# Two of four forgetting heads in query halves, and TensorE in the program's order from the merge on

## The chip, the core and the metric

One NeuronCore of a Trainium2 chip runs the whole program. It has a matrix engine (TensorE, PE in the profile), a vector engine (VectorE, DVE), an activation engine (ScalarE, ACT), GpSimd (POOL), and a queue engine that issues the transfers (SyncE, SP). Each engine works through its own list of instructions. The metric is device microseconds of one execution, the median of three runs.

## The reference, cut to what matters

```python
def token_mixer(h, w_in, b_forget, w_up_a, w_up_b, w_out):
    z = h @ w_in
    qa, ka, va, qb, kb, vb, fz, gza, gzb = jnp.split(z, SPLIT_POINTS, axis=-1)
    ya = dilated_mixture(qa, ka, va) @ w_up_a             # branch A: 12 heads, 3 groups of 4
    yb = forgetting_attention(qb, kb, vb, fz, b_forget) @ w_up_b   # branch B: 4 heads
    merged = jax.nn.sigmoid(gza) * ya + jax.nn.sigmoid(gzb) * yb
    return merged @ w_out

def one_block(args):                                      # of branch B: 128 queries of every head
    i, qi, Fi = args
    s = jnp.einsum('bqhd,bkhd->bhqk', qi, k).astype(jnp.float32) * scale
    s = s + (Fi[..., :, None] - F[..., None, :])
    qpos = i * BLOCK + jnp.arange(BLOCK)
    s = jnp.where(kpos[None, :] <= qpos[:, None], s, -jnp.inf)
    p = jax.nn.softmax(s, axis=-1)
    return jnp.einsum('bhqk,bkhd->bqhd', p.astype(v.dtype), v)
```

2048 tokens, 1024 channels, all in float32. Before `token_mixer` stands a normalisation, behind it a residual add, a gated feed-forward layer and a last normalisation.

## The kernel before

The program runs in stages: the input projection, the two attention branches with the merge, the output projection, and the feed-forward layer. The change lies in the second one.

**Branch A** (`branch_a`, `head_a`) handles one head after the other: scores, softmax without its division, sums. A head ends with its results in DRAM (`u_scr`, `den_scr`, `sta_scr`). **Branch B** (`branch_b`, `head_f`) handles a head in blocks of 128 queries. `half_tiles` loads the head's queries `qs`, keys in a high and a low part `kh` and `kl`, and values `vhl` (for keys 0 to 1023 packed into two tiles, `kk` and `qv`). `scores(cq, b)` handles one block of 128 queries, in segments of up to 512 keys: two matmuls into `psX` or `psZ`, one DVE instruction that adds the bias and takes the running maximum (the profile's L853, followed by a short read of the accumulator), then ACT's exponentials (L863). `sums(cq)` handles 256 queries. For every pair `kp` of key blocks it transposes four 128x128 pieces on PE into `psT` (L887), lets ACT copy them as the high part `ph` (L104) and DVE subtract to get the low part `pl` (L105), and then multiplies the values with both on PE into `psY` (L895), four matmuls in the order ph, pl, ph, pl. In this text four transposes, the copy, the subtraction and four matmuls are a block pair. A head's second half (queries 1024 to 2047) has 5, 6, 7 and 8 of them, so 26.

**Merge and first products.** When branch A is done, `merge_weights` turns its statistics into weights, through DRAM (`wrow`). `up(cp)` then handles a half of the 2048 tokens: it loads results of both branches and the weights into tiles `uw`, makes the operands `y` (split in high and low again), and multiplies them with `w_up_a` and `w_up_b` into `psZ` (L98 to L100: 12 matmuls a step), where DVE multiplies with the gates `gt` (L1017). `up(0)` needs every head's first half of queries, `up(1)` the second half.

**Order.** All of this is written as generators, and `together` draws steps from two of them in turn: each step yields a cost, a factor stretches it, and the generator with the lower clock goes next. Branch A against branch B goes with `PACE[0]`, and `up(0)` against what is left of B with `PACE[1]`. The framework's scheduler takes the instructions in that order as a priority and fixes each engine's own list when the program is built, by a model of its own; so an engine's list can differ from the order in which the code issues. Inside `tc.manual_schedule(engines={...})` the engine named there keeps the program's order.

Before, B runs all four heads over the first half of the queries and then all four over the second half. The merged stretch (up(0) with B) begins when the four first halves are done (`f_done` at 8), with the second halves to go, of which head 0's is nearly done and head 1's begun when branch A ends. Tiles are drawn from pools with a fixed number of slots: 11 of tag `big` (8 KiB a partition; q, k, v and y), 3 of `bigx` (`uw`), 2 buffers for each of `psX`, `psY`, `psZ`, `psT`.

## Time and profile before

| | us |
|---|---|
| median of three runs | 2924.74 (2924.5 to 2925.12) |
| the profiled execution, its own time | 2925.13 |
| its span, first to last instruction | 2923.4 |
| end of branch A (its last store is issued) | 1159.6 |
| end of branch B (its last product ends) | about 1375 |
| end of up(1) | about 1442 |

The time outside the span is 1.7 us. Times inside are counted from the span's start. The stage of the change is the stretch from 876 us, where the last products of the input projection give way to the two branches, to 1442 us. A profile's busy share of PE counts each matmul from its start to its modelled end, so two matmuls in flight overlap; the spacing of their starts tells what each costs.

### The profile page before, as it was taken

The numbers are of one execution on the slowest core, as the hardware profiler recorded it, in microseconds if no ns is written. First come the engines' busy times: TensorE is split into PE (matmuls) and PEld (weight loads), VectorE is DVE, ScalarE is ACT, GpSimd is POOL, SyncE is SP. The second block draws the span as 40 slices with busy tenths as digits, with TensorE's granted clock in tenths as the row PEclk, the third lists the DMA queues.
The fourth block names the chain that finished last, engine by engine and source line by source line (L and its number), as shares of the span: only waits on it lengthen the run. The fifth ranks groups of instructions, "written<-read, shape, count | busy, mean of one in ns | idle before, by whom it ended". The sixth has DMA issues, their size and how long they took to land.

```text
span 2923.4 us, 40639 instructions
## 1 busy us (share of the span) xinstructions
PE 2761.3 (94%) x13666; PEld 2286.0 (78%) x13666; DVE 2059.2 (70%) x4295; ACT 1378.0 (47%) x2722; POOL 184.3 (6%) x291
## 2 busy tenths in 40 slices
PE   5899999999999988787899999999999999989998
PEld 4689888978888877675677788888888888868876
DVE  7765578576547877886877866657755558786987
ACT  4654345344447767555255633334433335343543
POOL 0000000000002222342300000000000000000000
PEclk8999999999999999999899999999999999999999
DMA  7587476467858885965856654444522235685642
GB/s 252 155 218 226 130 214 197 152 173 203 247 182 288 271 207 165 277 214 179 287 174 206 211 169 134 136 159 126 173 80 83 80 114 180 211 259 170 219 152 98
DMA packets 527321, 538.89 MB, mean 184 GB/s; under 512 B 91876, under 2 KB 376956, under 8 KB 521212
## 3 DMA queue, kind: packets, MB, share of 16 engines
q1 hardware_dynamic: 527112, 536.30, 59.1%
q8 instruction: 107, 1.75, 0.3%
q14 instruction: 102, 0.84, 0.1%
HBM read 364.89 MB, written 171.29 MB: 183 GB/s over the span
## 4 chain that ended last, share of the span: by engine, by line
PE 48%; DMA 5%; DVE 4%; issue 1%; ACT 1%; SPq 0%; POOLq 0%; POOL 0%; DVEq 0%; ACTq 0%
PE psX L98 9%; PE psX L99 9%; PE psX L100 9%; PE psZ L98 5%; PE psZ L99 5%; PE psZ L100 5%; PE psY L99 2%; PE psY L98 2%; PE psY L100 2%; DMA uw<-wrow 1%; DMA wr<-in_w_up_b_dram 1%; PE psY L895 1%; DMA kl<-qk 0%; PE psX L851 0%; DMA h2sp<-pe 0%
## 5 line engine op out<-in xcount | busy, mean ns | idle before, releaser
L104 ACT ACTIVATE wh<-wt 128x512 fp32r<-128x512 f32 (+1 forms) x464 | 288.5, 623 | 630.8 <-PE psX L99 332.4
L105 DVE TENSOR_TENSOR wl<-wt,wh 128x512 fp32r<-128x512 f32 (+1 forms) x464 | 314.5, 681 | 258.4 <-ACT wh L104 240.4
L104 ACT ACTIVATE wh<-wr 128x512 fp32r<-128x512 f32 (+1 forms) x324 | 201.5, 623 | 454.1 <-PE psX L99 254.1
L105 DVE TENSOR_TENSOR wl<-wr,wh 128x512 fp32r<-128x512 f32 (+1 forms) x324 | 220.0, 680 | 193.1 <-ACT wh L104 172.2
L215 DVE TENSOR_TENSOR wt<-wr 128x512 f32<-128x512 f32 (+1 forms) x216 | 146.6, 679 | 11.9 <-DMA wr<-in_w_in_dram 5.6
L215 DVE TENSOR_TENSOR wt<-wr,wt 128x512 f32<-128x512 f32 (+1 forms) x216 | 147.1, 681 | 3.7
L242 ACT ACTIVATE u<-psX 128x512 f32<-128x512 f32 x216 | 125.6, 581 | 8.6 <-PE psX L100 7.6
L839 POOL TENSOR_SCALAR bi<-nf,F_col 128x512 f32<-128x512 f32 (+3 forms) x160 | 106.4, 667 | 260.3 <-DVE mx L853 210.5
L863 ACT ACTIVATE L<-L,nmf 128x512 f32<-128x512 f32 (+3 forms) x160 | 103.4, 648 | 27.1 <-DVE nmf L859 26.8
L104 ACT ACTIVATE ph<-psT 128x512 fp32r<-128x512 f32 (+1 forms) x126 | 71.3, 573 | 69.4 <-PE psT L887 67.4
L1123 DVE TENSOR_TENSOR ac<-psZ,u 128x512 f32<-128x512 f32 x88 | 60.5, 688 | 42.2 <-PE psZ L100 41.2
L105 DVE TENSOR_TENSOR pl<-psT,ph 128x512 fp32r<-128x512 f32 (+1 forms) x126 | 81.5, 653 | 9.8 <-ACT ph L104 9.4
L797 PE MATMUL psY<-pf,va 128*65 128x128 f32 (+1 forms) x408 | 78.9, 328 | 3.2 <-DVE nm L764 1.1
L769 ACT ACTIVATE L<-L,nm 128x128 f32<-128x128 f32 (+1 forms) x192 | 72.5, 450 | 18.9 <-DVE nm L764 17.6
L887 PE MATMUL psT<-ident,L 128*128 128x128 f32 x477 | 77.0, 281 | 1.4 <-ACT L L863 1.1
L761 DVE CUSTOM_DVE_ANT_0 L<-psX,bias 128x128 f32<-128x128 f32 (+1 forms) x192 | 64.1, 356 | 19.3 <-PE psX L759 11.0
L895 PE MATMUL psY<-pl,vhl 128*128 128x256 f32 x208 | 60.0, 315 | 12.8 <-DVE pl L105 10.9
L98 PE MATMUL psZ<-y,wu 128*128 128x512 f32 x128 | 54.2, 425 | 17.6 <-ACT y L104 10.6
L100 PE MATMUL psX<-f_A11h,wl 128*128 128x512 f32 x176 | 68.6, 390 | 0.5 <-DVE wl L105 0.5
L98 PE MATMUL psZ<-f_S4h,wh 128*128 128x512 f32 x176 | 68.7, 390 | 0.2 <-DVE ac L1123 0.2
L98 PE MATMUL psX<-f_A11h,wh 128*128 128x512 f32 x176 | 68.9, 391 | 0.0
L99 PE MATMUL psX<-f_A11l,wh 128*128 128x512 f32 x176 | 68.6, 390 | 0.0
(539 smaller groups left out, 8647.7 us busy)
## 6 DMA issues: line engine op xcount, KB each, us to landing
x<-x SPq DMA_DIRECT2D x192, 256.0 KB
wr<-in_w_ffn_in_dram SPq DMA_DIRECT2D x88, 512.0 KB
wr<-in_w_in_dram SPq DMA_DIRECT2D x64, 512.0 KB
qk<-sh SPq DMA_DIRECT2D x192, 128.0 KB
act<-ac SPq DMA_DIRECT2D x88, 256.0 KB
pc<-wfg SPq DMA_DIRECT2D x77, 256.0 KB
qk<-st SPq DMA_DIRECT2D x128, 128.0 KB
wa<-in_w_ada_dram SPq DMA_DIRECT2D x64, 256.0 KB
```

Of the source, the lines that this page charges most:

```text
L98: PE.matmul(o, lh, rh, start=first, stop=False, skip_group_check=True)
L99: PE.matmul(o, lh, rl, start=False, stop=False, skip_group_check=True)
L100: PE.matmul(o, ll, rh, start=False, stop=last, skip_group_check=True)
L104: A.activation(hi, src, AF.Copy)
L105: V.tensor_tensor(lo, src, raw(hi), op=ALU.subtract)
L215: V.tensor_tensor(v[i], *made[i](g, v), op=ALU.subtract)
L242: A.activation(t, o, AF.Copy, scale=1.0 if scale is None else scale)
L797: PE.matmul(uo[:65, qb_[0] * P:qb_[0] * P + w], va[:, 4 * u + kb_, :], pf[:, pos:pos + w], start=i_ == 0, stop=i_ == len(runs) - 1, skip_g ...
L839: G.tensor_scalar(bi[:, :e - sg], nf[sg // D][:, sg % D:sg % D + e - sg], 1.0, F_col[:, qb * NHB + h:qb * NHB + h + 1], op0=ALU.mult, op1= ...
L863: A.activation(Ls[cq, b, sg][:, :e - sg], Ls[cq, b, sg][:, :e - sg], AF.Exp, bias=nm, accum_out=dp[:, i:i + 1])
L887: PE.transpose(pt[:, n:n + P], Ls[cq, b, sg][:, kb * P - sg:kb * P - sg + P], ident)
L895: PE.matmul(uo[:, q0:256], vhl[:, kb, :], p_[:, 256 * i:256 * i + 256 - q0], start=(kp == 0 and i == 0 and j == 0), stop=(last and i == 1 ...
```

## The change

Heads 0 and 1 of branch B run over all 2048 queries at once, with their tiles loaded once; heads 2 and 3 keep the two halves. The list `FOX` sets the order: heads 0 and 1, the first halves of heads 2 and 3, their second halves. The merged stretch begins after the fourth entry, with two second halves to go; before, the second half of head 1 was still under way there too. Two paces change. And the code from there on is under `manual_schedule` for PE.

```diff
-PACE = (0.45, 1.5)
+PACE = (0.6, 1.25)
+
+FOX = ((None, 0), (None, 1), (0, 2), (0, 3), (1, 2), (1, 3))
...
-        qj, kj, half, n = 12 + h // 2, 14 + h // 2, h % 2, (part + 1) * D
+        qj, kj, half, n = 12 + h // 2, 14 + h // 2, h % 2, D if part == 0 else T
...
-            qs, vhl = qs[:, :D], vhl.rearrange("p (n e) -> p n e", e=P)
-        SP.dma_start(raw(qs), qk_rows(qj, half, 0)[:, n - D:n])
+            qs, vhl = qs if part is None else qs[:, :D], vhl.rearrange("p (n e) -> p n e", e=P)
+        SP.dma_start(raw(qs), qk_rows(qj, half, 0)[:, D if part else 0:n])
...
-        for part, h in [(p_, h) for p_ in range(2) for h in range(NHB)]:
+        for part, h in FOX:
             scores, sums = head_f(h, part)
-            for cq in range(4 * part, 4 * part + 4):
+            for cq in range(4 if part else 0, 4 if part == 0 else 8):
...
-            if h == NHB - 1:
+            if (part, h) in (FOX[-1], FOX[-3]):
                 yield from behind()
                 behind = None
...
-    together([(gb, 1.0)], lambda: f_done[0] >= 2 * NHB)
+    together([(gb, 1.0)], lambda: f_done[0] >= 12)
     tt_only[0] = "U"
-    gu = up(0)
-    together([(gu, PACE[1]), (gb, 1.0)])
-    for g in (gb, gu, up(1)):
-        for _ in g:
-            pass
+    with tc.manual_schedule(engines={PE.engine}):
+        gu = up(0)
+        together([(gu, PACE[1]), (gb, 1.0)])
+        for g in (gb, gu, up(1)):
+            for _ in g:
+                pass
```

On PE, in the merged stretch, the list of before had these rows in the second half of head 2 (`psY_13751` collects one group of 256 queries; `ph_13811` and `pl_13812` come from transposes further up, those of `psT_13819` are used further down):

```order
L895 MATMUL psY_13751<-pl_13799,vhl_13481 128x256
L895 MATMUL psY_13751<-ph_13798,vhl_13481 128x256
L895 MATMUL psY_13751<-pl_13799,vhl_13481 128x256
L895 MATMUL psY_13751<-ph_13811,vhl_13481 128x256
L887 MATMUL psT_13819<-ident_73,L_13501 128x128
L887 MATMUL psT_13819<-ident_73,L_13697 128x128
L887 MATMUL psT_13819<-ident_73,L_13501 128x128
L887 MATMUL psT_13819<-ident_73,L_13697 128x128
L851 MATMUL psX_13899<-kh_13478,qs_13480 128x512
L851 MATMUL psX_13899<-kl_13479,qs_13480 128x512
L895 MATMUL psY_13751<-pl_13812,vhl_13481 128x256
L895 MATMUL psY_13751<-ph_13811,vhl_13481 128x256
```

The changed kernel has these, in the same head (lines 887 and 895 are 890 and 898 there; `ph_14319` and `pl_14320` are made of `psT_14314`, right above them):

```order
L890 MATMUL psT_14314<-ident_73,L_13952 128x128
L890 MATMUL psT_14314<-ident_73,L_14137 128x128
L890 MATMUL psT_14314<-ident_73,L_13952 128x128
L890 MATMUL psT_14314<-ident_73,L_14137 128x128
L898 MATMUL psY_14233<-ph_14319,vhl_13492 128x256
L898 MATMUL psY_14233<-pl_14320,vhl_13492 128x256
L898 MATMUL psY_14233<-ph_14319,vhl_13492 128x256
L898 MATMUL psY_14233<-pl_14320,vhl_13492 128x256
L890 MATMUL psT_14327<-ident_73,L_13952 128x128
L890 MATMUL psT_14327<-ident_73,L_14137 128x128
L890 MATMUL psT_14327<-ident_73,L_13952 128x128
L890 MATMUL psT_14327<-ident_73,L_14137 128x128
```

What moved: the next pair's transposes, which stood ahead of a pair's products, now stand behind them. Steps of `up(0)` and blocks of scores stand between pairs, not inside one.

On SP, at the merge, the list of before reads as follows; `qs`, `kh` and `kl` are those of head 2's second half, and `wrow` are the merge weights:

```order
L973 DMA wrow<-mw 128x64 x3
L1011 DMA gt<-g_1_132 128x512
L990 DMA uw<-wrow 64x1024 x6
L1011 DMA gt<-g_1_164 128x512
L825 DMA nf<-nf 128x1024 x2
L1004 DMA wr<-in_w_up_a_dram 128x2x128
L1004 DMA wr<-in_w_up_b_dram 128x2x128
L1011 DMA gt<-g_0_135 128x512
L1011 DMA gt<-g_0_167 128x512
L984 DMA uw<-u_196 128x1024
L990 DMA uw<-wrow 64x1024 x2
L984 DMA uw<-u_198 128x1024
```

It goes on with two more of `uw<-wrow` and then `qs`, `kh`, `kl`. In the changed kernel:

```order
L976 DMA wrow<-mw 128x64 x3
L993 DMA uw<-wrow 64x1024 x6
L987 DMA uw<-u_196 128x1024
L993 DMA uw<-wrow 64x1024 x2
L987 DMA uw<-u_198 128x1024
L993 DMA uw<-wrow 64x1024 x2
L698 DMA qs<-qk_124 128x1024
L700 DMA kh<-qk_126 128x2048
L700 DMA kl<-qk_126 128x2048
L701 DMA vhl<-v_130 128x16x128
L987 DMA uw<-u_200 128x1024
L993 DMA uw<-wrow 64x1024 x2
```

What moved: little on SP itself; head 2's loads stand behind the same transfers of the merge. But on PE, between branch A's last products and head 2's first scores, before had 179 matmuls, nearly all of head 1's second half, and the changed kernel has 46 of head 3's first half.

## Rows read from the trace of the kernel before

**Rows 1.** The page: its head and its first row (busy us, share).

```profile
span 2923.4 us, 40639 instructions
...
PE 2761.3 (94%) x13666; PEld 2286.0 (78%) x13666; DVE 2059.2 (70%) x4295; ACT 1378.0 (47%) x2722; POOL 184.3 (6%) x291
```

**Rows 2.** Windows: length, busy PE, PEld, DVE, ACT, POOL, granted clock, DMA share, GB/s.

```profile
876.00:1160.00 284.00, 264.48 (x1824) 225.21 (x1823) 216.71 (x886) 212.25 (x500) 69.08 (x144) 0.99 0.77 237
1160.00:1249.00 89.00, 66.64 (x360) 53.03 (x359) 76.03 (x166) 45.94 (x112) 31.58 (x41) 0.92 0.89 254
1249.00:1376.00 127.00, 110.63 (x638) 89.96 (x637) 99.99 (x233) 71.45 (x168) 48.31 (x66) 0.99 0.59 186
1376.00:1442.00 66.00, 53.02 (x211) 41.41 (x212) 50.87 (x73) 18.51 (x32) 22.22 (x15) 0.87 0.93 319
1750.00:1800.00 50.00, 50.00 (x223) 41.40 (x222) 31.48 (x49) 17.58 (x31) 0.00 (x0) 1.00 0.46 153
```

**Rows 3.** SP queue in order of time behind the end of branch A.

```profile
1159.57 0.45 SPq L812 DMA_DIRECT2D u<-utok  x1
...
1188.34 0.32 SPq L984 DMA_DIRECT2D uw<-u  x1
...
1191.60 0.67 SPq L696 DMA_DIRECT2D qs<-qk  x1
...
1193.45 0.32 SPq L698 DMA_DIRECT2D kl<-qk  x1
```

**Rows 4.** PE in order of time, where the next head's keys arrive.

```profile
1207.55 0.50 PE L851 MATMUL psX<-kl,qs 128*128 128x512 f32 x1 [1.06 <-DMA kl<-qk]
```

**Rows 5.** All engines in order of time, around one block pair of head 3.

```profile
1371.97 0.60 PE L887 MATMUL psT<-ident,L 128*128 128x128 f32 x4
...
1372.32 0.36 PE L895 MATMUL psY<-pl,vhl 128*128 128x256 f32 x1
...
1372.60 1.18 ACT L104 ACTIVATE ph<-psT 128x512 fp32r<-128x512 f32 x2 [2.08 <-PE psT L887]
...
1373.23 1.16 DVE L105 TENSOR_TENSOR pl<-psT,ph 128x512 fp32r<-128x512 f32 x2 [1.30 <-ACT ph L104]
...
1373.25 0.39 PE L895 MATMUL psY<-ph,vhl 128*128 128x256 f32 x1
...
1373.98 0.39 PE L895 MATMUL psY<-pl,vhl 128*128 128x256 f32 x1 [0.34 <-DVE pl L105]
...
1374.32 0.28 PE L895 MATMUL psY<-pl,vhl 128*128 128x256 f32 x1
...
1374.44 0.28 PE L895 MATMUL psY<-ph,vhl 128*128 128x256 f32 x1
```

**Rows 6.** Groups of instructions, forms apart, of 1249:1376 us.

```profile
L887 PE MATMUL psT<-ident,L 128*128 128x128 f32 x188 | 29.6, 276 | 1.1 <-ACT L L863 1.1
L105 DVE TENSOR_TENSOR pl<-psT,ph 128x512 fp32r<-128x512 f32 x43 | 29.2, 681 | 2.3 <-ACT ph L104 2.2
L863 ACT ACTIVATE L<-L,nmf 128x512 f32<-128x512 f32 x38 | 27.0, 713 | 2.3 <-DVE nmf L859 2.2
...
L98 PE MATMUL psZ<-y,wu 128*128 128x512 f32 x52 | 21.5, 413 | 3.7 <-ACT wu L104 2.2 <-DVE gt L1017 1.2 <-DVE nmf L859 0.2
...
L853 DVE CUSTOM_DVE_ANT_0 L<-psX,bi,mx 128x512 f32<-128x512 f32 x24 | 17.8, 741 | 4.9 <-PE psX L851 2.7 <-issue 1.1 <-PE psT L887 0.6
...
L853 DVE DVE_READ_ACCUMULATOR2_ANT mx<- 128x1 f32 x45 | 3.6, 79 | 0.0
```

**Rows 7.** Who PE waited for, 1376:1442 us: us, times, longest.

```profile
PE psZ L98 <- ACT y L104: 10.6, 1, 10.6
```

**Rows 8.** Windows of 4 us (columns of rows 2): thin work, then a stop.

```profile
1357.00:1361.00 4.00, 1.84 (x16) 1.57 (x15) 0.53 (x2) 1.07 (x2) 0.00 (x0) 1.00 0.76 225
...
1381.00:1385.00 4.00, 0.00 (x0) 0.00 (x0) 2.88 (x4) 1.87 (x4) 0.00 (x0) 0.50 0.97 359
...
1389.00:1393.00 4.00, 3.59 (x9) 2.82 (x10) 4.00 (x5) 0.34 (x1) 2.97 (x2) 0.50 1.03 362
```

## The prediction

> **What bounds the kernel now.** I read the page first: PE is busy for 2761.3 us of a span of 2923.4 [rows 1], so the kernel is gained or lost in what PE does not do. Then windows over the stage of the change [rows 2]. Beside branch A (876 to 1160 us) PE is busy for 264.5 of 284 us, 93%. Behind it PE loses more: 66.6 of 89 us up to where head 1 of branch B ends (1249), 110.6 of 127 up to the end of B (1376), 53.0 of 66 in what is left of `up(1)`. DVE is no full bound in any of them (216.7 of 284, 76.0 of 89, 100.0 of 127, 50.9 of 66). So from the merge on the time is a matter of waits and of order, not of one engine's throughput. What a matmul really costs PE is the spacing of starts: 512 columns 50/223 = 0.224 us in a dense stretch [rows 2], the products of a block pair 0.12 each, four transposes 1372.32 - 1371.97 = 0.35 [rows 5].

> The rows that decide are those around one block pair late in head 3, where ACT and DVE are idle [rows 5]. The transposes start at 1371.97 and end at 1372.57; ACT copies from 1372.60; DVE subtracts from 1373.23, and the first product that needs its result starts at 1373.98. That is 1.41 us from the end of the transposes. Even there PE filled a part with products of the pair before (1372.32 and on) and waited only 0.34 us in front of that product. The rest of the pair's products follow at 0.12 us.

> **The change, part by part.** I count in the two lists of PE and price with the rows.

> Beside branch A: up to A's last product PE's list held 670 matmuls of branch B and now holds 886: 34 score matmuls, 90 transposes and 91 products more (and one small one). At PE's spacing that is 34 x 0.224 + 90 x 0.09 + 91 x 0.12 = 26 us. Lower bound: all of PE's idle 19.5 us there takes them up, +7. Upper bound by DVE: about 23 subtractions of 0.68 and 17 score segments of 0.74 + 0.08 [rows 6] and 4 us of small ones make 34 us, which at DVE's present share there (0.76) stretch the stage by 44. I take 26, because PE at 93% is the nearest to full.

> From A's end to head 2's second half: in the old kernel 89 us, in which PE finished head 1. Now PE has 46 matmuls of head 3's first half there, some 8 us, and then, in the program's order, nothing but head 2's scores. Their loads stand on SP behind the weights' whole chain through DRAM: A's last store was issued at 1159.57, `qs` at 1191.60, and the matmul that waited for `kl` started at 1207.55 [rows 3, 4], 48 us behind. The chain is the same in the new list. Lower bound: 32 us to the issue plus the 2.6 MB of `qs`, `kh`, `kl` at 319 GB/s (the fastest window of rows 2), 40. Upper bound: the 2.1 MB of `uw` ahead of them count too, at 254 GB/s, 50. I take 46, nearest to the row. So 89 becomes 46, a gain of 43 (bounds 39 to 49), with PE idle for some 38 us of it: SP, DVE and POOL have the merge to do, PE is what is late.

> The merged stretch: the new list has 52 block pairs there (200 transposes and 208 products), 56 score segments (112 matmuls) and 156 matmuls of `up(0)`; the old kernel did about as much from 1249 to 1376 (188 transposes by L887, 157 matmuls of `up` by three times L98's 52, 45 segments by the reads of the accumulator [rows 6]) in 127 us. In program order a pair's products stand right behind its transposes. By rows 5 a pair then takes 1373.98 - 1371.97 = 2.01 us to the first product that needs `pl`, and 0.46 for that one, two more and the start of the next transposes (1374.44), 2.47 us. 52 pairs are 128 us, of which 73 are PE waiting (52 x 1.41). What is queued behind the waiting product is everything else PE has: `up`'s matmuls and the scores are ready and cannot pass. The scores come in ten blocks of 3 to 9 segments; with two buffers of `psX` they go at DVE's pace, 0.74 + 0.08 for a full segment [rows 6], 0.70 over their widths as an estimate from that row: 40 us. Bounds: PE's own 112 x 0.224 = 25, and 46 with every segment at full price. `up`: 156 x 0.224 = 35. Four of the ten blocks are followed at once by transposes that need exponentials of the same block, three or four of 0.71 [rows 6], half of it hidden: 5. DVE has `up`'s products with gates and the preparation of `up(1)` beside the pairs, and a subtraction finds it busy now and then: 5. Sum 213, against 127: +86. Lower bound 128 + 25 + 35 = 188 (+61); upper bound with DVE in the way at every second pair by 0.7 us, 18, and the scores at 46: about 240 (+113).

> The rest of `up`: 228 matmuls behind B's end instead of 174, 54 x 0.224 = 12 us more; but 36 of them are left over from `up(0)` and fill 8 of the 10.6 us for which PE waited for `y` [rows 7]. +4, bounds 0 and +12.

> Costed at nothing: the ten transfers that heads 0 and 1 no longer repeat (4.2 MB), which lay beside PE at 93%; if they were not hidden, 4.2 MB at 237 GB/s, 18 us of one queue spread over 284, bounds what they give back. From 1442 us on PE's list is the same but for a few rows.

> Sum: 26 - 43 + 86 + 4 = +73. On the profiled execution's 2925.1 that is **2998 us**; that execution lies 0.4 us above the median of the runs, so nothing is added. All lower bounds together give +19 (2944), all upper ones +130 (3055).

> **The rivals.** *The clock falls in the merged stretch.* PE works for under half of each pair, in short pieces. [...] If the stretch ran at 0.50, PE's own part, 200 x 0.09 + 208 x 0.12 + 156 x 0.224 = 78 us, would double: 3076. [...]

> *No empty stretch.* Head 2's loads come early enough that its scores follow head 3's 46 matmuls at 10 us: 36 us less, 2962. For it: the weights' chain runs through SP, DVE and ACT, and DVE has less other work beside it than in the old kernel, where it served head 1's second half (76.0 of 89 us busy [rows 2]). Against: the `uw` tiles ahead of them wait for a slot, and in the old trace that set the issue (`uw<-u` at 1188.34, `qs` at 1191.60 [rows 3]).

> *Faster: the pairs overlap after all.* If PE's wait inside a pair were filled as in the old list, the merged stretch would stay at 127 us and the change would bring 26 - 43 + 4 = -13: 2912. It decides at a merged stretch of 140 us, so at (140 - 40 - 35 - 10)/52 = 1.06 us a pair. PE's own part of a pair is 0.35 + 4 x 0.12 = 0.83, so its wait would have to be under 0.23 us instead of 1.41. Against it: the list, in which nothing stands between transposes and products, and the 1.41 us of rows 5, measured with ACT and DVE free.

> **How the numbers follow.** Forecast 0.72; clock 0.08; no empty stretch 0.09; overlap 0.08; a sum of the terms at their lowest, with the gap shorter too, near nothing 0.03. Differences under 0.2% (6 us) a measurement of this kernel can't tell from no change. The first three cases are slower: 0.89; same 0.03; faster 0.08. The range begins at 2945, which is the sum with every term at its lower bound and takes in the case without an empty stretch, and ends at 3050, 5 us short of every upper bound at once. Left out are the overlap, the sum near nothing and most of the clock's case, 0.18 together: 2945 to 3050.

> **What would show it.** PE's waits in the merged stretch: 52 times for `pl` (DVE, L105) of 0.7 us and as often for `ph` (ACT), some 70 us in all. A hole of 30 us or more in PE behind A's end, ended by `kh` or `kl`. Merged stretch 190 to 240 us long. Branch A's end 10 to 40 us later. Wait for `y` at `up(1)` under 5 us. The prediction is wrong if the merged stretch stays under 150 us, or if A's end moves by more than 60.

## The result, and the profile after

The changed kernel takes **3056.5 us** (median of 4 runs, 3055.55 to 3057.12), against 2924.6 for the one before (median of 4 runs): a ratio of 1.0454, 95% interval 1.0435 to 1.0472. It is 132 us slower. I had forecast the sign, and +73; 3056.5 lies 6.5 us above the top of my range.

The first rows of the page after: the span, the busy time of each engine, and the granted clock of its forty slices in tenths.

```profile
span 3054.4 us, 40634 instructions
...
PE 2825.7 (93%) x13666; PEld 2318.3 (76%) x13666; DVE 2068.5 (68%) x4295; ACT 1376.6 (45%) x2722; POOL 179.3 (6%) x291
...
PEclk8999999999999997577899999999999999999999
```

PE's busy time grew by 64 us over [rows 1] with the same 13666 matmuls. That can be the clock (a matmul of 512 columns counts 0.63 us at a clock of 0.50 and 0.40 at 1.00, rows of 1360.72 and 1362.03 below), or matmuls that overlap less. The last row shows where the clock was low: slices 16 to 20, 1145 to 1527 us, with 0.7, 0.5, 0.7, 0.7, 0.8. Windows over the stage (columns as in [rows 2]; A's last store is issued at 1182.67, head 2's first scores start at 1216.86, B's last product ends at 1504.5):

```profile
876.00:1183.00 307.00, 292.60 (x2051) 252.49 (x2050) 246.12 (x967) 237.67 (x570) 82.74 (x168) 0.99 0.67 209
1183.00:1216.80 33.80, 4.58 (x33) 3.77 (x30) 17.20 (x31) 4.52 (x11) 0.00 (x0) 0.62 0.77 213
...
1216.80:1504.40 287.60, 198.20 (x681) 137.43 (x682) 127.78 (x272) 82.27 (x191) 57.93 (x80) 0.68 0.39 120
```

Against [rows 2]: branch A ends 23 us later; the 89 us behind it have become 34; the 127 us of the merged stretch have become 288, at a mean clock of 0.68. From B's end to the end of the span it is 1550 us, before 1548. The stretch is the loss.

What PE waited for in it (engine, line, releaser: us, times, longest):

```profile
PE psY L898 <- ACT ph L106: 44.9, 52, 2.6
PE psX L854 <- DMA kh<-qk: 28.7, 1, 28.7
PE psY L898 <- DVE pl L107: 15.2, 27, 2.8
PE psX L854 <- DVE mx L856: 15.0, 26, 2.1
PE psY L875 <- DVE den L873: 8.7, 3, 4.3
```

Fifty-two times for `ph`, once in every block pair, and 60 us for `ph` and `pl` together. The 28.7 us are the hole behind A, ended by `kh`. Two block pairs, from the start of their transposes to the start of the next ones, PE in order of time, the first at the low clock, the second at the full one:

```profile
1234.18 1.06 PE L890 MATMUL psT<-ident,L 128*128 128x128 f32 x4
1235.98 0.58 PE L898 MATMUL psY<-ph,vhl 128*128 128x256 f32 x1 [0.75 <-ACT ph L106]
1236.71 0.58 PE L898 MATMUL psY<-pl,vhl 128*128 128x256 f32 x1
...
1237.51 1.05 PE L890 MATMUL psT<-ident,L 128*128 128x128 f32 x4
...
1499.82 0.60 PE L890 MATMUL psT<-ident,L 128*128 128x128 f32 x4
1501.10 0.39 PE L898 MATMUL psY<-ph,vhl 128*128 128x256 f32 x1 [0.69 <-ACT ph L106]
1501.82 0.38 PE L898 MATMUL psY<-pl,vhl 128*128 128x256 f32 x1 [0.34 <-DVE pl L107]
...
1502.28 0.50 PE L890 MATMUL psT<-ident,L 128*128 128x128 f32 x3
```

At the full clock a pair takes 1502.28 - 1499.82 = 2.46 us; I had worked out 2.47. At the low clock it takes 1237.51 - 1234.18 = 3.33. Two windows, and PE in order of time where the clock rises and falls again (at 1361.57 a matmul of 512 columns goes from 0.6 to 0.4 us, at 1368.55 one of 256 from 0.4 to 0.6):

```profile
1216.80:1296.70 79.90, 46.87 (x130) 31.05 (x130) 42.94 (x81) 22.24 (x53) 15.00 (x21) 0.50 0.78 231
1296.70:1504.40 207.70, 151.32 (x553) 106.38 (x552) 84.84 (x191) 60.03 (x138) 42.93 (x59) 0.75 0.24 77
...
1360.72 0.63 PE L101 MATMUL psZ<-y,wu 128*128 128x512 f32 x1
...
1362.03 0.40 PE L102 MATMUL psZ<-y,wu 128*128 128x512 f32 x1
1362.27 0.60 PE L890 MATMUL psT<-ident,L 128*128 128x128 f32 x4
1363.61 0.39 PE L898 MATMUL psY<-ph,vhl 128*128 128x256 f32 x1 [0.75 <-ACT ph L106]
...
1366.08 0.38 PE L898 MATMUL psY<-ph,vhl 128*128 128x256 f32 x1 [0.69 <-ACT ph L106]
...
1368.55 0.58 PE L898 MATMUL psY<-ph,vhl 128*128 128x256 f32 x1 [0.69 <-ACT ph L106]
```

For its first 80 us the stretch stays at 0.50; from 1297 on the clock goes up and down between 0.50 and 1.00, with a mean of 0.75 over 208 us. Each of its eight rises comes inside or right at the end of a step of `up`, twelve matmuls of 512 columns back to back, and the first step begins only at 1292.3 us. It falls again behind such a step, in the rows above in the third of three pairs, with no wait over 0.75 us on the way.

### The profile page after: what moved, and what is told of

It is laid out like the page before. It is cut to its first block, busy times and chain, and to the rows that moved or that the text cites. A ratio compares the mean times of both kernels' runs of the same rounds, so it can differ in the third digit from the quotient of the medians.

```text
span 3054.4 us, 40634 instructions
## 1 busy us (share of the span) xinstructions
PE 2825.7 (93%) x13666; PEld 2318.3 (76%) x13666; DVE 2068.5 (68%) x4295; ACT 1376.6 (45%) x2722; POOL 179.3 (6%) x291
## 4 chain that ended last, share of the span: by engine, by line
PE 51%; DMA 6%; DVE 6%; ACT 4%; issue 3%; SPq 1%; POOL 0%; POOLq 0%; DVEq 0%; ACTq 0%
PE psX L100 8%; PE psX L101 8%; PE psX L102 8%; PE psZ L100 5%; PE psZ L101 4%; PE psZ L102 4%; PE psY L100 2%; PE psY L101 2%; PE psY L102 2%; PE psY L898 2%; ACT L L866 1%; PE psY L799 1%; DMA uw<-wrow 1%; DVE pl L107 1%; PE psT L890 1%
## 5 line engine op out<-in xcount | busy, mean ns | idle before, releaser
L898 PE MATMUL psY<-ph,vhl 128*128 128x256 f32 x248 | 86.9, 358 | 48.2 <-ACT ph L106 47.0
L106 ACT ACTIVATE ph<-psT 128x512 fp32r<-128x512 f32 (+1 forms) x110 | 62.3, 568 | 146.0 <-PE psT L890 145.6
L107 DVE TENSOR_TENSOR pl<-psT,ph 128x512 fp32r<-128x512 f32 (+1 forms) x110 | 71.5, 650 | 76.2 <-ACT ph L106 76.0
L898 PEld LDWEIGHTS psY<-ph,vhl 128*128 128x128 f32 x248 | 56.0, 226 | 67.9 <-ACT ph L106 65.3
L898 PE MATMUL psY<-pl,vhl 128*128 128x256 f32 x248 | 84.9, 364 | 19.9 <-DVE pl L107 15.9
L898 PEld LDWEIGHTS psY<-pl,vhl 128*128 128x128 f32 x248 | 55.8, 225 | 36.5 <-DVE pl L107 35.5
L1020 DVE TENSOR_TENSOR gt<-psZ,gt 128x512 f32<-128x512 f32 x64 | 43.7, 686 | 45.5 <-PE psZ L102 43.6
L854 PE MATMUL psX<-kh,qs 128*128 128x512 f32 (+3 forms) x56 | 29.3, 523 | 44.0 <-DMA kh<-qk 28.7
```

The costliest lines, as they stand in the source:

```text
L106: A.activation(hi, src, AF.Copy)
L107: V.tensor_tensor(lo, src, raw(hi), op=ALU.subtract)
L898: PE.matmul(uo[:, q0:256], vhl[:, kb, :], p_[:, 256 * i:256 * i + 256 - q0], start=(kp == 0 and i == 0 and j == 0), stop=(last and i == 1 ...
```

## The experiments

All runs side by side. "A to B" is the time from the issue of A's last store to the end of B's last product in the profiled execution, with the mean granted clock in it; the ratio is to the kernel before, run on the same chip.

| run | what differs | us | ratio (95%) | A to B, us | clock |
|---|---|---|---|---|---|
| before | | 2924.6 | | 215.4 | 0.96 |
| after | | 3056.5 | 1.0454 (1.0435 to 1.0472) | 321.8 | 0.67 |
| e1_free | after, PE's order left to the scheduler | 2922.3 | 1.0004 (0.9994 to 1.0015) | 187.3 | 0.85 |
| e2_manual_only | before, program's order on PE | 3115.0 | 1.0662 (1.0637 to 1.0688) | 410.6 | 0.65 |
| e3_ahead | after, transposes one pair ahead | 2971.2 | 1.0174 (1.0154 to 1.0194) | 236.0 | 0.78 |
| e4_fill | after, pairs filled with zeros | 3030.2 | 1.0374 (1.0352 to 1.0396) | 294.5 | 0.84 |
| e5_hole | after, hole filled with zeros | 3062.3 | 1.048 (1.0459 to 1.0501) | 325.1 | 0.69 |
| e6_hole_fill | after, both filled | 3034.9 | 1.0384 (1.0364 to 1.0405) | 294.7 | 0.89 |
| e7_free_early | e1, head 2 loaded early | 2899.8 | 0.9925 (0.9906 to 0.9943) | 168.3 | 0.92 |
| e8_free_pace | e1, paces of before | 2924.8 | 1.0016 (1.0004 to 1.0028) | 210.7 | 0.91 |
| e9_manual_early | after, head 2 loaded early | 3035.6 | 1.0395 (1.0379 to 1.0411) | 298.3 | 0.69 |
| e10_two_ahead | e9, transposes two pairs ahead | 2951.6 | 1.0104 (1.009 to 1.0118) | 215.8 | 0.81 |
| e11_early_pace | e7, paces of before | 2924.8 | 1.0013 (1.0004 to 1.0022) | 209.5 | 0.90 |
| e12_fill_unweighted | e4, up(0) without the weights | 3035.1 | 1.0383 (1.0359 to 1.0407) | 284.9 | 0.84 |

**Which part of the change costs.** First the changed kernel without the manual schedule:

```diff
-    with tc.manual_schedule(engines={PE.engine}):
-        gu = up(0)
-        together([(gu, PACE[1]), (gb, 1.0)])
-        ...
+    gu = up(0)
+    together([(gu, PACE[1]), (gb, 1.0)])
+    ...
```

> The changed kernel with its new head order and paces, but without the manual schedule for TensorE. Theory (serial block pairs cost about 75 us of waits, and the low granted clock that comes with them about 75 more): pairs overlap again, the stretch from head 2's first scores to the end of B falls from 287 us to 130 to 160, the clock there is back above 0.95; 2900 to 2930 us. Rival 1 (the new head order itself is dear: the hole behind branch A starts a low clock that stays): 2970 us or more, clock in that stretch still under 0.8. Rival 2 (the waits alone, clock a side effect): 2975 to 2990.

2922.3 us, level with the kernel before. The stretch is back at 153 us and a clock of 0.91 (I had expected above 0.95), PE's waits for `pl` at 3.9 us in all:

```profile
1188.00:1217.60 29.60, 0.55 (x6) 0.40 (x4) 12.68 (x17) 1.53 (x3) 0.00 (x0) 0.56 0.75 221
1217.60:1370.30 152.70, 130.31 (x693) 106.27 (x694) 121.20 (x274) 80.22 (x191) 65.63 (x81) 0.91 0.70 222
```

So the whole 134 us are the program's order on PE. The low clock isn't the kind of work either: the 200 transposes and 208 products of the pairs are the same. The new head order is worth nothing by itself, neither with the new paces nor with those of before (e8_free_pace, ratio 1.0016), and with the new ones it carries a hole of 29 us. The counterpart gives the kernel before nothing but that order:

```diff
-    gu = up(0)
-    ...
+    with tc.manual_schedule(engines={PE.engine}):
+        gu = up(0)
+        ...
```

> The kernel before with the manual schedule on TensorE alone; head order and paces as before. It leaves no hole behind branch A, since head 1's second half stands there. Theory (serial pairs bring waits and by themselves the low clock): about 70 pairs in series, 1.41 us of wait each, stretch from A's end to B's end 330 us against 216, granted clock 0.6 to 0.8; 3020 to 3060 us. Rival 1 (the clock falls only because of the hole): clock above 0.95, 2955 to 2975 us. Rival 2 (the manual order costs only together with the new head order): 2930 to 2940.

3115.0: dearer than I had said, since A to B took 411 us and not 330. The clock answers the more interesting question, whether it needs the hole in order to fall. Here there is no hole, since head 1's second half follows A's end at once. PE at the first serial pair, and the clock before and behind it:

```profile
1162.86 0.60 PE L887 MATMUL psT<-ident,L 128*128 128x128 f32 x4
1164.15 0.39 PE L895 MATMUL psY<-ph,vhl 128*128 128x256 f32 x1 [0.69 <-ACT ph L104]
1164.87 0.49 PE L895 MATMUL psY<-pl,vhl 128*128 128x256 f32 x1 [0.34 <-DVE pl L105]
...
1155.00:1165.00 10.00, 7.93 (x56) 6.38 (x54) 4.24 (x7) 4.97 (x9) 0.00 (x0) 1.00 0.27 58
1165.00:1170.00 5.00, 2.74 (x11) 2.04 (x11) 1.96 (x9) 1.09 (x4) 0.00 (x0) 0.50 0.41 113
```

The pair waits 0.69 and 0.34 us, and 0.69 is the longest idle time of PE since 1150 us. From 1165 on, for 44 us, the clock stands at 0.50 (in every window of 5 us up to 1205; 0.56 in the next). So here it fell behind waits of 0.69 and 0.34 us, without a stop, as it did at 1368 us in the changed kernel behind waits of 0.75 us at most.

**The order inside a pair.** The program itself issues the next pair's transposes ahead of the present pair's products, in the merged stretch alone:

```diff
+            ahead = 1 if tt_only[0] == "U" else 0
+            got = []
             for kp in range(cq + 1):
...
-                pt = psT("F")
+                while len(got) <= min(kp + ahead, cq):
+                    got.append(turned(len(got)))
+                ops, last = got[kp], kp == cq
```

> The changed kernel, still in the program's order from the merge on, but the program there issues the transposes of the next pair ahead of the products of the present one. Theory (serial pairs): a pair takes about 1.41 us at the full clock instead of 2.47, 52 pairs give back 45 to 55 us, and the thicker work brings back a part of the clock, 20 to 70 us; 2935 to 2990 us, 2955 the likeliest. Rival 1 (hole behind A sets the clock, thin work doesn't matter): clock stays under 0.7 up to 1300 us and the gain is about 50, 3005. Rival 2 (DVE or ACT is the bound of the stretch and not the order): within 15 us of 3056.

2971.2, 85 us back. PE's waits inside pairs fell from 60 to 21 us, and the clock of the stretch rose from 0.68 to 0.81:

```profile
PE psX L854 <- DVE mx L856: 15.6, 26, 1.7
PE psY L904 <- DVE pl L107: 11.7, 22, 1.9
PE psY L904 <- ACT ph L106: 9.4, 11, 1.4
...
1217.00:1418.30 201.30, 152.33 (x681) 115.13 (x682) 126.12 (x272) 81.06 (x191) 62.69 (x80) 0.81 0.54 170
```

39 us of waits are gone, but 86 of the stretch. In the rest, the higher clock and matmuls that overlap more can't be told apart in this run.

**The clock by itself.** Five matmuls of zeros in each pair, which change no order and no dependence:

```diff
+                for d_ in range(5 if tt_only[0] == "U" else 0):
+                    PE.matmul(uo[:, :256], zero, vhl[:, 0:2, :],
+                              start=(kp == 0 and d_ == 0), stop=False, skip_group_check=True)
                 for i, kb in enumerate((2 * kp, 2 * kp + 1)):
```

> The changed kernel with five more matmuls of 256 columns in every serial pair, between its transposes and its first product; their weights are zeros, so they add nothing to the sums. They fill about 0.6 us of the wait for the copy and leave order and dependences as they are. Theory (two costs, waits and clock): waits stay, the granted clock of the stretch rises from 0.68 to above 0.9, time 2980 to 3020 us. Rival 1 (waits alone made the loss; the low clock is a side effect without a price): the added work costs or is hidden, 3055 to 3075. Rival 2 (the clock is low because of the hole, not of the thin work): clock stays near 0.7, 3060 to 3090.

3030.2: more work on PE and 26 us less time, as the theory of two costs wants, though 10 us outside its numbers and with a clock of 0.87, not above 0.9. A filled pair, and the windows of the stretch (whole, its first 82 us, the rest):

```profile
1308.20 0.60 PE L892 MATMUL psT<-ident,L 128*128 128x128 f32 x4
1308.55 0.84 PE L899 MATMUL psY<-vhl,zero 128*128 128x256 f32 x5
1309.54 0.39 PE L904 MATMUL psY<-ph,vhl 128*128 128x256 f32 x1 [0.15 <-ACT ph L106]
1310.27 0.39 PE L904 MATMUL psY<-pl,vhl 128*128 128x256 f32 x1 [0.34 <-DVE pl L107]
...
1310.73 0.60 PE L892 MATMUL psT<-ident,L 128*128 128x128 f32 x4
...
1217.70:1476.80 259.10, 193.26 (x941) 146.15 (x942) 127.37 (x272) 82.43 (x191) 59.84 (x80) 0.87 0.44 133
1217.70:1300.00 82.30, 52.51 (x198) 37.58 (x198) 46.36 (x92) 22.56 (x54) 20.57 (x26) 0.66 0.78 228
1300.00:1476.80 176.80, 140.75 (x745) 108.57 (x744) 81.01 (x181) 59.87 (x138) 39.27 (x55) 0.96 0.28 89
```

A filled pair takes 1310.73 - 1308.20 = 2.53 us, 0.07 more than an empty one at the same clock, and the clock rises to 0.87, in the part from 1300 on to 0.96. Order and dependences are unchanged, so this gain is the clock's. Counted from each start on PE to the next, the pairs, zeros included, became 16 us shorter and `up` 13. The first 82 us stay low, and I suspected the hole. Two runs fill it, one with the pairs as they are, one with the pairs filled too:

```diff
+        o = ps("X")
+        for d_ in range(300):
+            PE.matmul(o[:, :P], zero, zero, start=(d_ == 0), stop=(d_ == 299), skip_group_check=True)
         gu = up(0)
```

> The changed kernel with 300 small matmuls of zeros on TensorE (128 columns, into a score buffer that nothing reads) ahead of head 2's second half, so that TensorE works through the hole behind branch A; nothing else differs. Theory (serial pairs are thin work and bring the low clock by themselves): the clock is 1.00 when head 2's scores begin, falls within the first pairs, and the gain is the 10 to 25 us by which the first scores and pairs run faster: 3030 to 3050 us. Rival (the stop behind A sets the low clock, and thin work only fails to lift it): clock above 0.9 in the whole stretch, 2980 to 3000 us.

> Both fillings at once: zeros in the hole and five matmuls of zeros in every serial pair. Theory (the stretch costs 213 us at the full clock, waits included, and what it took beyond that with the pairs filled, 259, is the low clock of its first 82 us): stretch 215 to 230 us, clock above 0.95; 2985 to 3002 us. Rival (the rest is waits on DVE for scores and denominators, at any clock): stretch 245 to 260, 3015 to 3030 us.

3062.3 and 3034.9: nothing gained by filling the hole, with or without filled pairs. The test is not clean, since the zeros ended 4 and 5 us before `kh` came, and the clock fell to 0.50 in what was left of the hole (in the first run at 1218.8 us, by its mean of 0.88 from 1215 to 1220; in the second it was 0.64 from 1220 to 1225). A window of the first run in the zeros, and its first score:

```profile
1195.00:1217.00 22.00, 22.00 (x199) 22.00 (x198) 9.05 (x11) 1.15 (x2) 0.00 (x0) 1.00 0.68 188
...
1221.73 0.80 PE L856 MATMUL psX<-kh,qs 128*128 128x512 f32 x1 [3.95 <-DMA kh<-qk]
```

With the pairs filled too, the first 77 us of the stretch ran at 0.72 and not at 0.66, and all of it took 257 us, not the 215 to 230 of my theory. A cleaner case is the changed kernel with head 2's tiles loaded ahead of the merge, so that its scores begin beside A:

```diff
+    pre[2, 1] = half_tiles(2, 1)
     merge_weights()
```

> The changed kernel, manual schedule kept, with the tiles of head 2's second half allocated and loaded ahead of the merge weights, so that no hole precedes the serial pairs. Theory (thin work sets the low clock by itself; the hole costs its 29 us and no more): hole gone, clock of the stretch still 0.6 to 0.8, 3020 to 3035 us. Rival (the stop sets the clock): the clock stays above 0.9 and the time falls to 2960 to 2985 us.

3035.6, 21 us less than the changed kernel, with the clock of A to B still at 0.69. The rival, that the stop sets the clock of the whole stretch, is out: without the hole the mean clock is as low (0.69, with it 0.67). The 21 us are less than the 29 of the hole. The clock's first long fall there, at 1202.8 us (a mean of 0.78 from 1200 to 1205, 0.50 in the next 5 us), comes in a wait of 3.9 us for `pl`, so it is the kernel before with the manual order and the row at 1368 us that show a fall behind waits under 1 us.

**What is left of the stretch.** At 0.87 the stretch still took 259 us where I had 213. On DVE's queue stand products of `up(0)` that wait for the weights' transfers (28.0 us of waits, first row below), ahead of the reductions of the scores. I took that wait away:

```diff
-                V.tensor_tensor(uu, uu, wb, op=ALU.mult)
+                V.tensor_tensor(uu, uu, uu if cp == 0 else wb, op=ALU.mult)
```

> As the run with five matmuls of zeros in every serial pair, but the products that prepare the operands of up(0) multiply each tile with itself and not with the merge weights (so branch A's part of the first half is not weighted); the same number of DVE instructions, and they no longer wait for the weights' transfers. Open is why the stretch from head 2's first scores to B's end still took 259 us there where 213 were worked out at the full clock. Theory (these waits stand at the head of DVE's queue, and scores and subtractions behind them): the stretch falls to 225 to 240 us, PE's waits for score maxima from 19 to under 10 us. Rival 1 (low clock at the start alone): 250 to 260 us. In either case head 2's loads may be issued earlier, since the slots of the operands come free earlier; that shortens the hole and not the stretch. Time 2975 to 3010 us by the theory, 3015 or more by the rival.

It did not come out: the stretch, from 1204.74 to 1469.4, took 265 us. DVE's waits for transfers at that place were not all gone, some only changed their name. Its waits from 1185 to 1300 us, first with the filled pairs alone, then in this run:

```profile
DVE uw L1001 <- DMA uw<-wrow: 28.0, 9, 6.6
...
DVE uw L1001 <- DMA uw<-wrow: 7.5, 4, 2.7
DVE uw L1001 <- DMA uw<-u: 6.9, 4, 3.5
DVE uw L1001 <- DMA uw<-rc: 4.4, 1, 4.4
```

They fell from some 31 to 19 us, and PE's waits for score maxima from 19.1 to 13.6, not under 10. The stretch became no shorter, so this run can't tell whether the queue on DVE is the cause. It stays open. (Its total time does not help: from B's end to the end of the span it took 1563 us, against 1548 with the filled pairs alone, and why was not followed up.)

**Versions that might win.** Without the manual schedule the hole of 29 us stands alone and can be had. The same early load there:

> The new head order and paces, no manual schedule, and the tiles of head 2's second half allocated and loaded ahead of the merge weights. Theory (the hole of 29 us behind A in the run without the manual schedule comes only from those loads standing behind the weights' chain on SP): hole under 5 us, 2885 to 2905 us, faster than the kernel before. Rival 1 (the stretch is bound by DVE and transfers behind the hole, and what is gained there is lost until the end of the first products): 2912 to 2924. Rival 2 (the earlier loads hold slots that branch A wants): A ends later by 10 us or more, no gain.

**2899.8 us**, 0.75% faster than the kernel before (0.56 to 0.94%). SP issues `qs` at 1143.46 now, 40 us before A's last store instead of 24 us behind it (1207.29 against 1183.02 without the early load), and A ends where it ended (rows of SP in order of time):

```profile
1143.46 0.92 SPq L698 DMA_DIRECT2D qs<-qk  x1
...
1183.03 0.45 SPq L814 DMA_DIRECT2D u<-utok  x1
```

Of the 29 us, 22 come back in the time. The paces, by themselves and with the early load:

> The new head order without the manual schedule and with the paces of the kernel before (0.45 and 1.5). Theory (the paces only shift work of branch B between the stage beside A and the merged stretch): A ends 10 to 25 us earlier, the hole is filled with first halves of heads 2 and 3, and the time is within 12 us of 2922. Rival (the paces decide): more than 20 us slower than with the new ones.

> Early loads without the manual schedule as in the run that beat the kernel before, but with the paces of the kernel before. Theory (the paces shift work over A's end and the hole was the price of the new ones): with the old paces there was a smaller hole to fill, so the gain is smaller, 2908 to 2922 us. Rival (early loads and old paces add up): under 2895 us.

2924.8 both times. With the old paces A ends at 1159 and 1162 and A to B takes 211 and 210 us; with the new ones 187 without and 168 with the early load. So the paces only shift work over A's end, until the hole is gone; then the new ones are 25 us better. With the old paces the early load brings nothing, less than the smaller gain that I had expected.

Last, the program's order made as good as I could, two pairs ahead and early loads:

> Manual schedule kept, early loads as in the run before this one, and in the program the transposes run two pairs ahead of the products. Theory (the loss is the order inside the pairs, not that a program's order was given at all): a pair near 1 us, clock above 0.9 behind the first segments, 2905 to 2930 us. Rival (only a list in which first products and scores also move between pairs does as well as the scheduler's): 2935 to 2965 us.

2951.6, the rival's case: waits for `ph` and `pl` in front of products are down to 2.5 us, but PE now stands in front of the next transposes, of score blocks and of `y`:

```profile
PE psX L854 <- DVE mx L856: 22.9, 22, 3.2
PE psT L887 <- DVE pl L107: 19.7, 12, 5.1
...
PE psZ L100 <- ACT y L106: 10.9, 1, 10.9
```

In the scheduler's list, matmuls of `up` and scores stand in those places. With the same early loads that list takes 2899.8 us, so the best program's order that I tried is still 52 us behind it.

## Why the prediction was right or wrong

**Beside branch A:** +26 forecast, +23 measured. PE's busy time grew by 28 us (264.5 to 292.6); its idle time took up 5 of them (19.5 to 14.4), and the rest came on top, near the case that I chose.

**From A's end to head 2's scores:** 46 forecast, 34 measured. The mechanism is right (loads behind the weights' chain, a hole ended by `kh`); the term was 12 us too long. `qs` was issued 24 us behind A's last store and not 32, below my lower bound for that step; the other 4 us lie between the issue and the first score (SP in order of time):

```profile
1182.67 0.45 SPq L814 DMA_DIRECT2D u<-utok  x1
...
1206.40 0.53 SPq L698 DMA_DIRECT2D qs<-qk  x1
```

**The serial pairs:** the price at the full clock was right, 2.46 us a pair against 2.47, and there are 52 waits for `ph`. The 73 us of waits were wrong at any clock: the 1.41 us of a pair hold the first product with `ph`, which runs while DVE subtracts (in the last pair above the product starts at 1501.10, and the subtraction runs from 1501.08 for 0.69 us). At the full clock PE waits 0.69 + 0.34 = 1.03 us, 54 us in 52 pairs; 60 were measured, and only 27 waits for `pl`.

**The merged stretch as a whole: the step that failed.** 213 us forecast, 288 measured. I read [rows 8] so that thin work, 1.84 us of 4, leaves the clock at 1.00, and gave the fall of the clock 0.08. One window of 4 us said nothing about a stretch of 200 with the same pattern over and over; the kernel before with the manual order shows the fall behind the first serial pair, and in the changed kernel the clock was at 0.50 for the first 80 us. My rival put the price of a whole stretch at 0.50 at 78 us more, 291 us. It doubled what PE's work costs; the starts of `up`'s matmuls stand 0.43 us apart at 0.50 (1358.16 to 1358.59) and 0.23 at 1.00 (1361.80 to 1362.03), a little less than double. By the windows the clock stood at 0.50 for (1 - 0.68)/0.5 = 64% of the time; an estimate from that and the rival's 78 us, 0.64 x 78, is 50 us. PE's rows, counted from each start to the next, show where the 75 us lie:

| in the stretch | forecast, us | measured, us |
|---|---|---|
| 52 pairs with their waits | 128 | 170 |
| `up` | 35 | 51 |
| scores with their waits | 40 | 55 |
| small products of the denominators, with their waits | nothing | 9 |
| blocked by exponentials or by DVE, ends | 10 | 3 |

The 16 pairs at a clock of 1.00 took 2.47 us in the median, the 30 at 0.50 took 3.33 in the median and 3.69 in the mean. By these rows some 28 us of the pairs (30 x 0.86, and six pairs between the levels) and 13 of `up` (38 us in the run with the pairs filled) are the clock, so 40 to 50 of the 75 us by the two estimates. The other 25 to 35 lie in longer waits in pairs, in the scores and in the denominators; the last of these I had put at nothing. The run with the pairs filled leaves about as much: 26% of its stretch at 0.50 would cost about 20 us on top of 213, and the longer pairs 4, so 237, where 259 were measured. There PE waits 19.1 us for score maxima and 6.0 for denominators, in the changed kernel 15.0 and 8.7. Why they came to that was not settled.

**Tail:** +4 forecast, between B's end and the end of the span +1.5 measured.

**The rivals:** the case of the clock named the mechanism, at 0.08. That it put the stretch at 291 us, where 288 were measured, is luck: it took the clock to be at 0.50 throughout, which it was for 64% of the time, and longer waits made up the rest (PE's in the stretch: 60 us in pairs, 15.0 for score maxima, 8.7 for denominators). It said 3076 in all, and the other terms came out 3, 12 and 3 us lower. By the same errors the time lies only 6.5 us above my range, while the stretch lies 48 us above its upper bound of 240. The case without the empty stretch did not occur, nor did the overlap; that one is what the run without the manual schedule shows, with 187 us from A to B, though its stretch took 153 us and not 127, and so it came out at 2922 and not at 2912. **Costed at nothing:** what the ten transfers less (4.2 MB) brought, no run isolates; the new head order with the paces of before, which has them, is no faster than the kernel before (1.0016).

## What to carry to other kernels

Giving TensorE the program's order is only as good as the program's inner loop: where transposes, a copy, a subtraction and the products of one block stand in a row, every pass pays the way over two other engines, here 1.03 us of waits in a pair of 2.46 at a clock of 1.00. These short waits cost twice, once as waits (60 us for `ph` and `pl`) and once through the clock (0.68 in the stretch, 40 to 50 us by my two estimates), and even with transposes two pairs ahead that order lost 52 us to the scheduler's list. So price the stretch at both levels that the windows show, 1.00 and 0.50, and don't take a single window at the full clock as evidence. When a stretch behind a stage boundary starts with a hole, look for loads that stand in a queue behind something that they don't need; here allocating them earlier was worth 22 us without the manual schedule and 21 with it, and nothing with the paces of before.
